# Sums of squared activations stored by the first MLP product, and the last of seven products moved two products on

## The chip, the cores and the metric

The kernel runs on one core of a Trainium2 chip as one program. The metric is the device time of one execution in microseconds. The core's engines work at the same time, each through its own instructions in a fixed order: TensorE (PE in the profile) multiplies into eight PSUM banks, VectorE (DVE), ScalarE (ACT) and GpSimd (POOL) do elementwise work, and SyncE (SP) issues nearly all of the DMAs. An instruction starts when everything ahead of it on its engine has been started and its semaphores are reached, so an instruction that waits holds up all that stand behind it on its engine.

## What is computed

Two layers of a trunk on 1024 tokens of width 1024. Each ends in the same squared-ReLU MLP with 4096 hidden features, which is all that the change touches:

```python
def sqrelu_mlp(hn, w1, w2):
    return jnp.square(jax.nn.relu(hn @ w1)) @ w2
...
        hn = modulate(rms_norm(h, norm2_g[layer]), sh2, sc2)
        h = h + g2[:, None, :] * sqrelu_mlp(hn, mlp_w1[layer], mlp_w2[layer])
```

The first layer mixes tokens with a recurrent block, the second with chunked attention. All is float32; the result must be close to that of float32 arithmetic.

## The kernel before

**Precision.** Each float32 operand is split into a high part (rounded by ScalarE to the type that PE multiplies) and a low part (the difference, made by DVE or POOL). A product of two operands is then three matmuls, high by high, high by low and low by high (lines 241 to 243). Each takes a 128 x 128 block of weights and 512 columns.

**Seven products for eight.** Both matrix products of an MLP are cut into 2 x 2 blocks and multiplied with seven block products in place of eight. This takes sums: of the weight blocks (four instructions on POOL for each group of four loaded blocks, line 111), of the activations of the first product (made once), and of the hidden activations, the squared ReLUs, for the second product. The hidden sums are called T1 to T4, the blocks used as they are B11, B22, B21 and B12. The list `PROD` gives the order of the seven products: which of the four weight units, which half of it, which moving operand, which of three PSUM banks, and whether the bank starts anew. A bank isn't finished with its first product: each further product adds to what lies in it, after the sum so far has been read out. So product after product in a bank has to wait for the read of the one before.

**First product.** Features come in 16 pairs of 128-feature blocks. Pairs 0 and 1 are multiplied plainly, pairs 2 to 15 by the function `quad`, with 4 blocks to a product, 84 matmuls to a pair. ScalarE copies the first three reads of a bank out, DVE adds and squares the rest (lines 998 to 1004). The four finished half tiles of a pair (B11 and B12 side by side in one tile, `ca`, and B21 and B22 in the other, `cb_`) go to DRAM, to the array `hid`, in two DMAs of 512 KB (line 944), issued while the next pair is worked on.

**Second product.** 16 steps, listed in `STEPS`: three short ones of one, two and three pairs, then 13 of four pairs each, every time `quad` with the hidden activations as moving operand. Each step needs a new group of weights, and each full step one new pair of `hid`. The stream of loads fetches that pair in two DMAs of 512 KB, lets ACT and DVE split B11 and B22, lets POOL make T3, T1 and T2 in place (line 359), splits those and B21, and then has POOL make T4. After every product DVE adds the bank, scaled, to the residual `h` (line 1027). A tail of plain products closes what the steps leave.

**What sets the order.** `Stream` holds all weight and `hid` loads in one list. It loads as far as seven raw tiles of 512 KB (`ws`) allow, and splits as far as eight tiles of split weights (`wh`) and a number of operand tiles (`cap["a"]`, up to 30) are free; `pump` is called when a unit is done. All operands, the tiles `ca` and `cb_` and the residual share 38 tiles (`s`). The residual is out of these tiles during the first product and comes back with `reload`, 512 KB each (line 987): blocks 2 to 5 while pairs 8 to 11 are worked on, 6, 7, 0 and 1 at its end. The function `some` puts loads for the modulation vectors of later stages (512 KB each, `in_ada` and `in_kvada`, with one long DVE instruction, line 274) among the units, in the first layer only. A scheduler places the instructions of each engine when the kernel is built, so the fixed order of an engine is seen in the built program and not in the source.

## Time and profile before

| | us |
|---|---|
| runs: median (lowest to highest) of three | 2520.14 (2513.54 to 2522.19) |
| the profiled execution, its own time | 2512.75 |
| its span, first to last instruction | 2511.0 |
| first product of layer 0, the seven-product part | about 640 to 855 |
| second product of layer 0 | about 855 to 1180 |
| first product of layer 1 | about 1950 to 2155 |
| second product of layer 1 | about 2155 to 2500 |

Engines over the span: PE 2323.5 us busy (93%), DVE 1821.6 (73%), ACT 1114.5 (44%), POOL 1112.0 (44%). A busy PE is not PE at its full pace, since matmuls overlap and their ends are modelled; the number of matmuls in a stretch says more. Where nothing holds PE, a matmul of 512 columns starts every 0.226 us.

### The profile page before, as it was taken

The numbers are of one execution on the slowest core, as the hardware profiler recorded it, in microseconds if no ns is written. First come the engines' busy times: TensorE is split into PE (matmuls) and PEld (weight loads), VectorE is DVE, ScalarE is ACT, GpSimd is POOL, SyncE is SP. The second block draws the span as 40 slices with busy tenths as digits, with TensorE's granted clock in tenths as the row PEclk, the third lists the DMA queues.
The fourth block names the chain that finished last, engine by engine and source line by source line (L and its number), as shares of the span: only waits on it lengthen the run. The fifth ranks groups of instructions, "written<-read, shape, count | busy, mean of one in ns | idle before, by whom it ended". The sixth has DMA issues, their size and how long they took to land.

```text
span 2511.0 us, 31516 instructions
## 1 busy us (share of the span) xinstructions
PE 2323.5 (93%) x11764; PEld 1941.9 (77%) x11764; DVE 1821.6 (73%) x2328; ACT 1114.5 (44%) x1808; POOL 1112.0 (44%) x767
## 2 busy tenths in 40 slices
PE   4989888989999989899999999999999999999998
PEld 3767666867888767667799998998887888677777
DVE  8879888678766798776765557997386655887674
ACT  5567665244333333333444218997153333443331
POOL 3535335346343366553211027875046332566550
PEclk9989987999999999999999999999999999999999
DMA  7323344223554543334333300013213342533332
GB/s 292 115 81 83 103 138 151 75 72 118 178 191 167 172 152 121 114 122 139 126 118 126 102 5 12 12 35 112 99 34 125 116 141 101 172 101 102 100 105 93
DMA packets 103402, 283.74 MB, mean 113 GB/s; under 512 B 12016, under 2 KB 17264, under 8 KB 103248
## 3 DMA queue, kind: packets, MB, share of 16 engines
q1 hardware_dynamic: 101952, 277.40, 33.6%
q10 hardware_dynamic: 1296, 4.33, 0.5%
q8 instruction: 92, 1.51, 0.3%
q14 instruction: 62, 0.51, 0.1%
HBM read 219.82 MB, written 50.33 MB: 108 GB/s over the span
## 4 chain that ended last, share of the span: by engine, by line
PE 48%; DVE 22%; DMA 9%; ACT 8%; POOL 7%; issue 6%; SPq 0%; POOLq 0%; DVEq 0%; ACTq 0%
PE b L242 15%; PE b L243 14%; PE b L241 14%; DMA ws<-hid 5%; POOL ws L359 5%; DVE s L175 4%; DMA ws<-in_ada_dram 2%; DVE wl L175 2%; DVE s L1027 2%; POOL ws L111 2%; DVE ws L274 2%; ACT s L174 1%; PE b L1334 1%; ACT s L1304 1%; DVE s L274 1%
## 5 line engine op out<-in xcount | busy, mean ns | idle before, releaser
L242 PE MATMUL b<-s,wh 128*128 128x512 f32 x2540 | 1008.6, 398 | 62.8 <-DVE s L247 35.1
L241 PE MATMUL b<-s,wh 128*128 128x512 f32 x2540 | 995.8, 399 | 65.6 <-DVE s L1027 39.2
L243 PE MATMUL b<-s,wl 128*128 128x512 f32 (+1 forms) x2312 | 911.5, 397 | 12.4 <-DVE wl L175 12.3
L241 PEld LDWEIGHTS b<-s,wh 128*128 128x128 f32 x2540 | 481.6, 190 | 202.1 <-DVE s L1027 56.2
L242 PEld LDWEIGHTS b<-s,wh 128*128 128x128 f32 x2540 | 484.0, 191 | 180.4 <-DVE s L247 38.3
L243 PEld LDWEIGHTS b<-s,wl 128*128 128x128 f32 (+1 forms) x2312 | 440.3, 190 | 113.8 <-DVE wl L175 17.4
L111 POOL TENSOR_TENSOR ws<-ws,ws 128x512 f32<-128x512 f32 (+3 forms) x180 | 283.1, 1573 | 489.0 <-DMA ws<-in_w_dram 277.9
L174 ACT ACTIVATE wh<-ws 128x1024 fp32r<-128x1024 f32 (+4 forms) x324 | 303.5, 941 | 356.8 <-PE b L243 165.4
L175 DVE TENSOR_TENSOR wl<-ws,wh 128x1024 fp32r<-128x1024 f32 (+3 forms) x224 | 301.4, 1348 | 110.5 <-PE b L242 54.9
L174 ACT ACTIVATE s<-ws 128x512 fp32r<-128x512 f32 x230 | 136.5, 626 | 374.9 <-POOL ws L359 244.2
L175 DVE TENSOR_TENSOR s<-ws,s 128x512 fp32r<-128x512 f32 x230 | 199.2, 885 | 137.8 <-ACT s L174 137.0
L241 PE MATMUL b<-wh,s 128*128 128x256 f32 x768 | 216.7, 284 | 4.3 <-ACT s L473 2.2
L243 PE MATMUL b<-wh,s 128*128 128x256 f32 x768 | 213.2, 284 | 5.3 <-DVE s L474 5.1
L242 PE MATMUL b<-wl,s 128*128 128x256 f32 x768 | 216.7, 284 | 0.0
L359 POOL TENSOR_TENSOR ws<-ws,ws 128x512 f32<-128x512 f32 x96 | 153.1, 1595 | 131.0 <-DVE s L175 128.5
L1027 DVE SCALAR_TENSOR_TENSOR s<-b,mod,s 128x512 f32<-128x512 f32 x248 | 181.4, 741 | 37.1 <-PE b L243 37.1
L175 POOL TENSOR_TENSOR wl<-ws,wh 128x1024 fp32r<-128x1024 f32 (+2 forms) x40 | 106.2, 2660 | 218.0 <-ACT wh L174 218.0
L274 DVE CUSTOM_DVE_ANT_0 ws<-ws,cb,vec 128x1024 f32<-128x1024 f32 x68 | 101.8, 1501 | 94.9 <-DMA ws<-in_ada_dram 94.9
L241 PEld LDWEIGHTS b<-wh,s 128*128 128x128 f32 x768 | 147.8, 193 | 5.1 <-ACT s L473 2.9
L243 PEld LDWEIGHTS b<-wh,s 128*128 128x128 f32 x768 | 145.7, 193 | 6.3 <-DVE s L474 5.7
L242 PEld LDWEIGHTS b<-wl,s 128*128 128x128 f32 x768 | 147.8, 193 | 0.2 <-issue 0.2
L274 DVE CUSTOM_DVE_ANT_0 s<-s,cb,vec 128x1024 f32<-128x1024 f32 x44 | 79.2, 1826 | 36.1 <-DMA s<-in_ada_dram 31.0
(173 smaller groups left out, 3246.5 us busy)
## 6 DMA issues: line engine op xcount, KB each, us to landing
ws<-in_w_dram SPq DMA_DIRECT2D x216, 256.0 KB
hid<-s SPq DMA_DIRECT2D x64, 512.0 KB
ws<-hid SPq DMA_DIRECT2D x64, 512.0 KB
ws<-in_ada_dram SPq DMA_DIRECT2D x56, 512.0 KB
s<-in_ada_dram SPq DMA_DIRECT2D x40, 512.0 KB
ws<-in_w_in_dram SPq DMA_DIRECT2D x22, 512.0 KB
hsp<-s SPq DMA_DIRECT2D x32, 256.0 KB
s<-hsp SPq DMA_DIRECT2D x16, 512.0 KB
```

The source lines that it names most:

```text
L111: G.tensor_tensor(out=out, in0=in0, in1=in1, op=op)
L174: nc.scalar.activation(out=hi[:rows, :n], in_=src, func=AF.Copy)
L175: self.lo_engine.tensor_tensor(out=lo[:rows, :n], in0=src, in1=hi[:rows, :n].bitcast(F32), op=ALU.subtract)
L241: PE.matmul(ps, ah, bh, start=start, stop=False, skip_group_check=more)
L242: PE.matmul(ps, ah, bl, start=False, stop=False, skip_group_check=more)
L243: return PE.matmul(ps, al, bh, start=False, stop=stop, skip_group_check=more).ins
L274: V.tensor_tensor_reduce(out=t, in0=t, in1=cb, op0=ALU.mult, op1=ALU.add, scale=1.0, scalar=bias, accum_out=dst)
L359: G.tensor_tensor(out=out, in0=in0, in1=in1, op=ALU.subtract)
L1027: V.scalar_tensor_tensor(out=t, in0=ps, scalar=g2[:, m : m + 1], in1=t, op0=ALU.mult, op1=ALU.add)
L1304: A_.activation(out=p[:, lo:640], in_=p[:, lo:640], func=AF.Exp, scale=-1.0, bias=m, accum_out=s1)
L1334: PE.transpose(ps[:, x, e * 128 : (e + 1) * 128], ptile[e][:, col : col + 128], ident)
```

## The change

It has four parts.

1. **The sums are made where the activations are made.** `hid` has eight blocks for a pair in place of four. When the last product of a pair is read, the two tiles go to DRAM as they are; then POOL makes T3, T1, T2 and T4 in place with the same four subtractions, and both tiles go to DRAM again. So a pair is stored with four DMAs of 512 KB. The second product loads the seven operands of a pair in four DMAs, three of 512 KB with two operands each and one of 256 KB, and splits each as it comes, without a POOL instruction between.
2. **The order of the seven products.** B21 comes ahead of T3, and the last product, T4, is held back: class `Quads` does it after the first two products of the next pair or step.
3. **Engines.** For the pairs 0 to 3 in the second product POOL and not DVE makes the low parts of the loads that end with T3 and T4.
4. **Placement.** Only blocks 2 and 3 of the residual come back during the first product, at pairs 10 and 11; six are fetched at its end. The twelve `some` loads in the second product are in the twelve steps from the second full one on; before, three of them were in the three short steps.

```diff
-        (1, 1, "B22", 1, False), (2, 0, "T3", 0, False), (2, 1, "B21", 2, True),
+        (1, 1, "B22", 1, False), (2, 1, "B21", 2, True), (2, 0, "T3", 0, False),
         (3, 0, "T4", 0, False)]
+
+HID = ["B11", "T2", "T1", "B22", "B21", "T3", "T4", "B12"]
+HLOADS = [("B11", "T1"), ("T2", "B22"), ("B21", "T3"), ("T4",)]
...
-            self.lo_engine.tensor_tensor(out=lo[:rows, :n], in0=src,
-                                         in1=hi[:rows, :n].bitcast(F32), op=ALU.subtract)
+            (it["eng"] or self.lo_engine).tensor_tensor(
+                out=lo[:rows, :n], in0=src, in1=hi[:rows, :n].bitcast(F32), op=ALU.subtract)
...
-    hid = dp.tile([16, 128, 4, HALF], F32, name="hid")
+    hid = dp.tile([16, 128, 8, HALF], F32, name="hid")
...
     def pair(p):
...
+        its = []
+        for nms in HLOADS:
+            i, n = HID.index(nms[0]), len(nms)
+            d = HID.index(nms[-1]) - i if n > 1 else 1
+            src = hid[p][:, i : i + d * (n - 1) + 1 : d]
+            its.append(ws.item([(0, n * HALF, src)], [(x * HALF, HALF, True) for x in range(n)],
+                               to="a", eng=G if p < 4 and nms[-1] in ("T3", "T4") else None))
+        return its
...
-            if j:
+            if p0 > 0:
                 some(1)
...
+        def end(self):
+            if self.late is not None:
+                late, self.late = self.late, None
+                self.product(6, *late)
+
+        def step(self, *a):
+            a = (a[0], [bank() for _ in range(3)], *a[1:])
+            for x in range(6):
+                self.product(x, *a)
+                if x == 1:
+                    self.end()
+            self.late = a
...
-            for t, x in ((ca, 0), (cb_, 2)):
-                nc.sync.dma_start(hid[p][:, x : x + 2], t.rearrange("p (a b) -> p a b", a=2))
+            f = "p (a b) -> p a b"
+            nc.sync.dma_start(hid[p][:, 0:8:7], ca.rearrange(f, a=2))
+            nc.sync.dma_start(hid[p][:, 3:5], cb_.rearrange(f, a=2))
+            a, b = hs(0), hs(1)
+            for out, in0, in1 in ((cb_[:, a], ca[:, b], cb_[:, a]), (ca[:, b], ca[:, b], ca[:, a]),
+                                  (ca[:, a], ca[:, a], cb_[:, a]), (cb_[:, b], cb_[:, b], ca[:, a])):
+                G.tensor_tensor(out=out, in0=in0, in1=in1, op=ALU.subtract)
+            nc.sync.dma_start(hid[p][:, 1:3], ca.rearrange(f, a=2))
+            nc.sync.dma_start(hid[p][:, 5:7], cb_.rearrange(f, a=2))
...
-            def after(x):
-                if x == 1 and stored is not None:
-                    store(*stored)
+            def after(x, p=p, ca=ca, cb_=cb_):
+                if x == 6:
+                    store(p, ca, cb_)
...
-            if p in (8, 9, 10, 11):
-                reload(p - 6)
-        store(*stored)
+            quads.step([ws.next() for _ in range(4)], 4, nrm.op, read, after)
+            if p in (10, 11):
+                reload(p - 8)
+        quads.end()
         ws.cap["a"] = 30
         ws.pump()
-        for k in (6, 7, 0, 1):
+        for k in (4, 5, 6, 7, 0, 1):
             reload(k)
```

Three places show how the instructions move. In the changed kernel the line numbers differ: 113 is the weight sums (111 before), 142 the loads of the stream (137), 953 the subtractions in `store` (359 in `pair` before), 948 and 949 the stores of a pair's two tiles as they are (944), 954 and 955 their second stores, 998 the reload (987), 177 the low parts (175). A name such as `ws110_4538` is a tile and its number; `ws` are the raw loaded tiles.

**POOL in the first product.** Before, eight instructions in a row that are two groups of weight sums:

```order
L111 TENSOR_TENSOR ws110_4538<-ws111_4540,ws108_4535 128x512
L111 TENSOR_TENSOR ws108_4535<-ws111_4540 128x512
L111 TENSOR_TENSOR ws109_4537<-ws110_4538,ws111_4540 128x512
L111 TENSOR_TENSOR ws109_4537<-ws110_4538,ws109_4537 128x512
L111 TENSOR_TENSOR ws116_4673<-ws117_4675,ws114_4670 128x512
L111 TENSOR_TENSOR ws114_4670<-ws117_4675 128x512
L111 TENSOR_TENSOR ws115_4672<-ws116_4673,ws117_4675 128x512
L111 TENSOR_TENSOR ws115_4672<-ws116_4673,ws115_4672 128x512
```

Now, in the same stage (`s522` and `s523` are `ca` and `cb_` of one pair):

```order
L953 TENSOR_TENSOR s523_4625<-s522_4624,s523_4625 128x512
L953 TENSOR_TENSOR s522_4624<-s522_4624 128x512
L953 TENSOR_TENSOR s522_4624<-s522_4624,s523_4625 128x512
L953 TENSOR_TENSOR s523_4625<-s523_4625,s522_4624 128x512
L113 TENSOR_TENSOR ws128_5004<-ws129_5006,ws126_5001 128x512
L113 TENSOR_TENSOR ws126_5001<-ws129_5006 128x512
L113 TENSOR_TENSOR ws127_5003<-ws128_5004,ws129_5006 128x512
L113 TENSOR_TENSOR ws127_5003<-ws128_5004,ws127_5003 128x512
L953 TENSOR_TENSOR s530_4766<-s529_4765,s530_4766 128x512
```

Between one group of weight sums and the next there stand now the four subtractions of a pair, the first of which waits for that pair's tiles to have landed in DRAM.

**POOL in the full steps of the second product.** Before, the sums of the hidden pair (line 359) and those of the weights are interleaved:

```order
L359 TENSOR_TENSOR ws230_7104<-ws229_7085,ws230_7104 128x512
L111 TENSOR_TENSOR ws226_7058<-ws227_7080,ws226_7058 128x512
L359 TENSOR_TENSOR ws229_7085<-ws229_7085 128x512
L359 TENSOR_TENSOR ws229_7085<-ws229_7085,ws230_7104 128x512
L359 TENSOR_TENSOR ws230_7104<-ws230_7104,ws229_7085 128x512
L111 TENSOR_TENSOR ws233_7210<-ws234_7232,ws231_7109 128x512
L111 TENSOR_TENSOR ws231_7109<-ws234_7232 128x512
```

Now only the weight sums are left, step after step:

```order
L113 TENSOR_TENSOR ws211_6540<-ws212_6559,ws209_6501 128x512
L113 TENSOR_TENSOR ws209_6501<-ws212_6559 128x512
L113 TENSOR_TENSOR ws210_6536<-ws211_6540,ws212_6559 128x512
L113 TENSOR_TENSOR ws210_6536<-ws211_6540,ws210_6536 128x512
L113 TENSOR_TENSOR ws220_6693<-ws221_6713,ws218_6654 128x512
```

**SP and POOL where the first product gives way to the second.** Before, on SP (`s575` and `s576` are the last pair's tiles, `hsp` is the residual in DRAM):

```order
L944 DMA hid_86<-s575_5556 128x1024
L137 DMA ws164_5731<-in_w2_dram 128x384
L137 DMA ws166_5734<-in_w2_dram 128x384
L137 DMA ws167_5775<-in_w2_dram 128x384 x2
L944 DMA hid_86<-s576_5557 128x1024
L137 DMA ws168_5790<-hid_86 128x1024
L137 DMA ws169_5804<-hid_86 128x1024
L137 DMA ws170_5812<-in_kvada_dram 128x1024
L987 DMA s594_5752<-hsp324_2446 128x1024
```

Now, on SP (`s573` and `s574` are the last pair's tiles, `s567` the second tile of the pair before it):

```order
L955 DMA hid_86<-s567_5476 128x1024
L998 DMA s592_5838<-hsp324_2446 128x1024
L998 DMA s593_5840<-hsp324_2446 128x1024
L142 DMA ws168_5810<-in_w2_dram 128x384
L998 DMA s594_5842<-hsp324_2446 128x1024
L998 DMA s595_5844<-hsp324_2446 128x1024
L998 DMA s596_5846<-hsp324_2446 128x1024
L998 DMA s597_5848<-hsp324_2446 128x1024
L142 DMA ws169_5865<-in_w2_dram 128x384 x2
L142 DMA ws170_5880<-hid_86 128x2x512
L949 DMA hid_86<-s574_5623 128x1024
L142 DMA ws171_5888<-hid_86 128x2x512
```

And on POOL at the same place (`ws166` to `ws169` are the weights of the step with three pairs, `s605` to `s607` low parts of pair 2's B21, T3 and T4):

```order
L113 TENSOR_TENSOR ws168_5810<-ws169_5865,ws166_5772 128x384
L113 TENSOR_TENSOR ws166_5772<-ws169_5865 128x384
L953 TENSOR_TENSOR s574_5623<-s573_5622,s574_5623 128x512
L953 TENSOR_TENSOR s573_5622<-s573_5622 128x512
L953 TENSOR_TENSOR s573_5622<-s573_5622,s574_5623 128x512
L113 TENSOR_TENSOR ws167_5806<-ws168_5810,ws169_5865 128x384
L177 TENSOR_TENSOR s605_5898<-ws172_5896,s605_5898 128x512
L953 TENSOR_TENSOR s574_5623<-s574_5623,s573_5622 128x512
L177 TENSOR_TENSOR s606_5901<-ws172_5896,s606_5901 128x512
L177 TENSOR_TENSOR s607_5906<-ws173_5904,s607_5906 128x512
L113 TENSOR_TENSOR ws167_5806<-ws168_5810,ws167_5806 128x384
```

The store of the last pair's second tile now stands on SP behind six reloads, and the last two weight sums of the three-pair step stand on POOL behind the last pair's subtractions, which wait for that store to have landed.

More of the change, by code (lines that the diff above doesn't have):

```diff
@@ L1044, in after @@
                     ws.free("a", n)
-            quad([ws.next() for _ in range(4)], p1 - p0, mov, lambda x, ps: add(*spots[x], ps),
-                 after)
+            quads.step([ws.next() for _ in range(4)], p1 - p0, mov,
+                       lambda x, ps, spots=spots: add(*spots[x], ps), after)
+        quads.end()
         its = [ws.next() for _ in range(3)]
```

77 lines of the change are left out of this document (28 added, 49 removed).

## The prediction

> **What bounds the kernel now.** I read the busy time of PE by stretches first, then the waits, then the groups of one stretch. The stretches (us, PE busy and matmuls, granted clock, DMA share, GB/s) of the two MLPs:
>
> ```profile
> 640.00:840.00 200.00, 200.00 (x884) 1.00 0.51 177
> 840.00:930.00 90.00, 78.60 (x309) 0.95 0.49 161
> 930.00:1180.00 250.00, 225.18 (x955) 1.00 0.38 122
> 1950.00:2140.00 190.00, 190.00 (x840) 1.00 0.35 121
> 2140.00:2230.00 90.00, 80.00 (x333) 1.00 0.47 151
> 2230.00:2470.00 240.00, 222.40 (x946) 0.99 0.31 98
> ```
>
> The first product (rows 1 and 4) is dense: 200/884 = 0.2262 us for a matmul. At that pace the matmuls of the other rows would need 69.9, 216.0, 75.3 and 214.0 us; what is over is 20.1 and 34.0 us in layer 0 and 14.7 and 26.0 in layer 1, together 94.8 us. The first of each pair is the boundary of the two products, the second the full steps. So nothing can be won in the first product, and at most 95 us (3.8%) in the second. The waits from 860 to 1170 (total, times, longest) say why:
>
> ```profile
> ACT s L174 <- POOL ws L359: 123.6, 39, 7.3
> POOL ws L359 <- DVE s L175: 60.7, 24, 4.9
> DVE s L175 <- ACT s L174: 56.9, 38, 4.5
> ACT s L174 <- DMA ws<-hid: 55.5, 18, 6.3
> PE b L241 <- DVE s L1027: 24.8, 23, 2.3
> ```
>
> PE waits for DVE's additions (last row), and these are late because they stand on DVE behind splits (line 175) that wait for ACT, which waits for POOL's hidden sums (line 359), which wait for DVE again. The groups from 930 to 1180 (count, busy, mean ns, idle before) show that no engine is full:
>
> ```profile
> L175 DVE TENSOR_TENSOR s<-ws,s 128x512 fp32r<-128x512 f32 x81 | 67.4, 848 | 58.1 <-ACT s L174 58.1
> L1027 DVE SCALAR_TENSOR_TENSOR s<-b,mod,s 128x512 f32<-128x512 f32 x81 | 59.4, 741 | 0.0
> L175 DVE TENSOR_TENSOR wl<-ws,wh 128x1024 fp32r<-128x1024 f32 x34 | 49.5, 1457 | 0.6 <-ACT wh L174 0.6
> L274 DVE CUSTOM_DVE_ANT_0 ws<-ws,cb,vec 128x1024 f32<-128x1024 f32 x8 | 14.2, 1775 | 0.0
> L175 DVE TENSOR_TENSOR wh<-ws,wh 128x512 fp32r<-128x512 f32 x12 | 12.2, 1016 | 0.0
> L359 POOL TENSOR_TENSOR ws<-ws,ws 128x512 f32<-128x512 f32 x34 | 56.1, 1650 | 45.0 <-DVE s L175 44.1
> L359 POOL TENSOR_TENSOR ws<-ws 128x512 f32<-128x512 f32 x11 | 17.6, 1603 | 0.3
> ```
>
> **Full steps of the second product.** The four hidden sums, (56.1 + 17.6)/11.25 = 6.6 us of POOL for a step, leave, and with them the ring DVE - ACT - POOL. What stays on DVE in a step: seven splits 5.9, seven additions 5.2, three long weight splits 4.4, a short one 1.0, in layer 0 one modulation row 1.8: 18.3 us, against 84 x 0.2262 = 19.0 us of PE. It fits, barely in layer 0, well in layer 1 (16.5). A bank's next product now comes two products, 24 matmuls or 5.4 us, after every read, where it was one, 2.7 us; an addition takes 0.74, so it may stand behind three splits and not hold PE. Against it: loads of `hid` grow from 1 to 1.75 MB a step, 0.75/19 us = 39 GB/s on top of 122; row 1 shows 177 carried without harm. I take 4 us left in each layer (nothing is left if DVE never blocks; with 1.5 us of blocking on a late load it passes 19.0 by 0.8, so 10 us over 12 steps), and 60 - 8 = 52 us gained.
>
> **First product.** POOL gets the four subtractions of a pair there, 28 pairs in the steps, and each pair two stores more. Groups from 640 to 840, then the last loads of a group as SP issued them and POOL's first sum after them (start, us):
>
> ```profile
> L111 POOL TENSOR_TENSOR ws<-ws,ws 128x512 f32<-128x512 f32 (+1 forms) x30 | 53.8, 1792 | 118.3 <-DMA ws<-in_w_dram 116.3 <-DVE wl L175 1.2
> ...
> L111 POOL TENSOR_TENSOR ws<-ws 128x512 f32<-128x512 f32 (+1 forms) x10 | 13.5, 1351 | 0.7 <-DMA ws<-in_w_dram 0.7
> ```
>
> ```profile
> 724.13 2.01 SPq L137 DMA_DIRECT2D ws<-in_w_dram  x3
> ```
>
> ```profile
> 728.88 1.76 POOL L111 TENSOR_TENSOR ws<-ws,ws 128x512 f32<-128x512 f32 x1 [11.57 <-DMA ws<-in_w_dram]
> ```
>
> Three instructions of 1.79 and one of 1.35 make 6.7 us for a group of sums, and as much for the subtractions: 13.4 of 19.0 us, so POOL isn't full. But a ring appears: subtractions, second store on SP, the weight loads behind it, the weight sums, and only then the next pair's subtractions. Its length: 6.7 + 6.7, from issue to sums 728.88 - 724.13 = 4.75 (3.7 if issued without gaps, 0.33 each), and the two stores of 512 KB ahead of the loads, 1.3 to 3.1 us at 338 GB/s (row below). That is 18.4 to 21.3 us against 19.0. I take 19.6, near the middle: 0.6 late a step, 8 us after 13 steps. About 7 of them are hidden: T4 ends three products (8.2 us) into a step, its read, the first stores and the subtractions take 2 + 4 + 6.7, the loads behind them 6, which is 8 us into the next step; two sums and the split (3.1 + 2.2) end at 13, and PE needs them at 19. I count 5 us lost over both layers, bounds 0 and 45 (2.3 us late a step in both). Apart from this, T4 at the side of the next pair costs nothing: the matmuls are the same, and its weights are the one `wh` tile of eight that seven others leave free.
>
> **The boundary.** Here three modulation loads leave (1.5 MB), and the hidden sums of the first pairs. What comes is the queue shown ahead: SP issues six reloads (3.1 MB, before 2.1) and only then the last pair's second tile. The drain rate of a full queue, and what a wait does to the clock:
>
> ```profile
> 870.00:880.00 10.00, 9.94 (x37) 7.65 (x36) 10.00 (x14) 4.69 (x9) 5.00 (x5) 0.84 0.71 232
> 880.00:890.00 10.00, 7.90 (x25) 5.30 (x24) 10.00 (x12) 2.83 (x5) 7.94 (x5) 0.83 0.92 338
> ```
>
> ```profile
> 867.86 1.04 PE L241 MATMUL b<-s,wh 128*128 128x512 f32 x2 [1.99 <-ACT s L174]
> ...
> 869.92 0.63 PE L243 MATMUL b<-s,wl 128*128 128x512 f32 x1
> ...
> 872.91 0.55 PE L242 MATMUL b<-s,wh 128*128 128x512 f32 x1
> ```
>
> Let zero be where PE would end the last T4 undelayed. From the previous pair's second stores, issued about 2 us ahead of zero, to the last tile there are 6.4 MB in SP's order (2 x 0.5 of stores, the ready tile 0.5, reloads 3.1, weights 0.6, `hid` 0.5, the tile 0.5): 19 us at 338 GB/s, so with some 2 us of start and finish it lands at about 19. POOL then makes three subtractions (4.9), the third weight sum (1.5), three low parts and the fourth subtraction (6), the fourth sum (1.3): 33. ACT (0.9) and DVE (1.2) split it: 35. PE needs that weight 68 matmuls after zero, at 15.4. So the boundary costs 20 us in a layer; the half speed after the last wait (seven starts 0.43 apart between the two last rows above, in place of 0.23) would add 1.4, which is within the rounding of this chain. Bounds: 9 if the reloads were drained ahead, 40 if the queue drains at 232 GB/s as from 870 to 880, in 28 us, and nine POOL instructions take 2.3 us as below. I take 20: the rate is from the nearest full queue. Now it costs 20.1 and 14.7, so the boundary gives nothing in layer 0 and takes 5 in layer 1.
>
> A page bears on this. The Trainium skill, "TensorE: Matmul & The Clock Gate", Part 1, says that the clock falls to half after an idle window of about 3.4 us. The trace shows half speed after a wait of 1.99 us already, so here short waits cost too; by the page only the two long ones would, about 1 us less in a layer.
>
> **Sum.** 94.8 - 2 x 20 - 8 - 5 = 42 us. The profiled execution took 2512.75 (span 2511.0), the runs 2513.54 to 2522.19, median 2520.14; the same 42 us off the median give **2478**.
>
> **Rivals.**
>
> A, *slower: the POOL ring sets the step of the first product.* Place: the subtractions between the weight sums. It decides from 21.4 us on: 2.4 x 13 - 7 = 24 us in each layer, the gain of the rest. For it: POOL and DVE seem to slow each other. The longest weight sum, and one DVE instruction in the dense stretches of layer 0 and of layer 1, twice as long in the second, where by my reading it falls together with POOL's sums:
>
> ```profile
> 709.22 2.37 POOL L111 TENSOR_TENSOR ws<-ws,ws 128x512 f32<-128x512 f32 x1 [10.94 <-DMA ws<-in_w_dram]
> ```
>
> ```profile
> L175 DVE TENSOR_TENSOR wh<-ws,wh 128x512 fp32r<-128x512 f32 x11 | 7.5, 684 | 0.0
> ```
>
> ```profile
> L175 DVE TENSOR_TENSOR wh<-ws,wh 128x512 fp32r<-128x512 f32 x10 | 13.9, 1391 | 0.0
> ```
>
> With subtractions of 2.3 us the ring is 9.2 + 6.7 + 4.5 + 2.2 = 22.6: 3.6 x 13 - 7 = 40 us a layer, 80 - 47 = 33 slower, **2553**. Against it: layer 1 has no modulation loads there, and 1.79 is a mean over such meetings already. Chance 0.08. The Trainium skill, "GPSIMD Engine Reference", Specifications, has POOL share SBUF interfaces with VectorE, in contention with DVE instructions that have two SBUF inputs. The rows agree (both are such instructions); by that rule the work moved is work moved beside DVE's squares and splits, and this rival is what it would come to.
>
> B, *the boundary takes the gain:* 40 us each: 95 - 80 - 8 = 7, **2513**, no change that can be told. For it: the upper bound's two conditions both occur in the trace; against: they would have to meet twice. 0.07.
>
> C, *DVE becomes the bound of the full steps.* Only 0.7 us are left to it in layer 0; with 2 us of blocked time a step in layer 0 and 1 in layer 1 beyond that, 22 us go: about 20 gained, **2500**. Against: the 58 us for which it waits for ACT hung on POOL. 0.13.
>
> D, *the boundary is cheap,* if six reloads drain early: 9 a layer, 95 - 18 - 8 = 69, **2451**. For it: the loads that went with `some`; against: SP's order, which can't let a reload pass. 0.15.
>
> **How the numbers follow.** My forecast has 0.57. 0.3%, or 7.6 us, is about what can be told from no change. Faster are mine, C and D: 0.85; B is the same: 0.07; A is slower: 0.08. The range 2446 to 2508 holds D to C with a few us of either side, leaving out A, B and tails.
>
> **What would show it.** Right: in the full steps over 218 matmuls in 50 us (now 955/250 x 50 = 191), no ACT wait for POOL at hidden operands, POOL about 13 us busy in 19 in the first product and PE still dense there. At the boundary two PE waits of 5 us or more, on weights whose sums stand behind the last pair's subtractions. Wrong: gaps of PE in the first product that recur with the pairs (A); full steps below 210 with DVE over 95% busy (C); a boundary of over 30 us (B) or under 12 (D).

## The result: 1.6% slower, and the profile after

The changed kernel took 2561.34 us (median of four runs, 2556.97 to 2564.88), the kernel before 2521.16 (2513.54 to 2522.98) beside it: a ratio of 1.0164 with a 95% interval of 1.0138 to 1.0191. The prediction said 2478. The two profiled executions have spans of 2511.0 and 2558.3 us, 47.3 apart. The medians are only 40.2 apart: the profiled execution of the kernel before (2512.75 us) is 8 us under the median of its runs, and no stretch below can be named for that part.

Where the 47.3 us lie is read from instructions that both programs have. The rows below are from the timelines of ACT and DVE of the kernel before: pair 14's first copy in layer 0, the first addition of the second full step, the last additions of the layer, and the same three in layer 1 (start, length in us).

```profile
819.83 0.60 ACT L998 ACTIVATE s<-b 128x512 f32<-128x512 f32 x1 [0.27 <-PE b L243]
931.25 0.74 DVE L1027 SCALAR_TENSOR_TENSOR s<-b,mod,s 128x512 f32<-128x512 f32 x1
1222.94 1.40 DVE L1027 SCALAR_TENSOR_TENSOR s<-b,mod,s 128x512 f32<-128x512 f32 x2
2119.66 0.60 ACT L998 ACTIVATE s<-b 128x512 f32<-128x512 f32 x1 [0.27 <-PE b L243]
2226.36 0.74 DVE L1027 SCALAR_TENSOR_TENSOR s<-b,mod,s 128x512 f32<-128x512 f32 x1
2507.18 0.75 DVE L1027 SCALAR_TENSOR_TENSOR s<-b,mod,s 128x512 f32<-128x512 f32 x1 [0.61 <-PE b L243]
```

And the same instructions of the changed kernel:

```profile
868.35 0.60 ACT L1009 ACTIVATE s<-b 128x512 f32<-128x512 f32 x1 [0.32 <-PE b L245]
993.96 0.74 DVE L1037 SCALAR_TENSOR_TENSOR s<-b,mod,s 128x512 f32<-128x512 f32 x1
1278.93 1.40 DVE L1037 SCALAR_TENSOR_TENSOR s<-b,mod,s 128x512 f32<-128x512 f32 x2
2180.58 0.60 ACT L1009 ACTIVATE s<-b 128x512 f32<-128x512 f32 x1 [0.27 <-PE b L245]
2296.51 0.74 DVE L1037 SCALAR_TENSOR_TENSOR s<-b,mod,s 128x512 f32<-128x512 f32 x1
2554.52 0.75 DVE L1037 SCALAR_TENSOR_TENSOR s<-b,mod,s 128x512 f32<-128x512 f32 x1 [0.61 <-PE b L245]
```

The stretches between these rows, and what the change added to each (the last two pairs of a first product, 14 and 15, are counted with the boundary):

| stretch | before, us | changed, us | added, us |
|---|---|---|---|
| up to pair 14 of layer 0 (its first product) | 819.8 | 868.4 | +48.5 |
| boundary of layer 0, with the first full step | 111.4 | 125.6 | +14.2 |
| the other full steps and the tail, layer 0 | 291.7 | 285.0 | -6.7 |
| from there to pair 14 of layer 1 | 896.7 | 901.7 | +4.9 |
| boundary of layer 1 | 106.7 | 115.9 | +9.2 |
| the other full steps and the tail, layer 1 | 280.8 | 258.0 | -22.8 |

So the gain is there, most of it in layer 1, and the loss has one large place, which layer 1 does not share: the first product of layer 0. In layer 1 that product loses 4.6 of the 4.9 us, all of it between the first copies of pairs 2 and 5 (54.9 us against 50.3 before); from there on its pairs are 19.0 us apart, as before. The windows of the changed kernel show the same (us; then busy time and count of PE, PEld, DVE, ACT, POOL; granted clock, DMA share, GB/s):

```profile
640.00:890.00 250.00, 221.88 (x919) 179.78 (x920) 178.46 (x168) 66.12 (x91) 145.15 (x88) 0.94 0.55 189
890.00:994.00 104.00, 83.34 (x305) 63.40 (x304) 72.57 (x87) 37.03 (x62) 57.26 (x44) 0.86 0.66 219
994.00:1246.00 252.00, 235.80 (x1000) 191.48 (x1000) 178.74 (x234) 88.85 (x125) 57.40 (x42) 0.97 0.52 164
1996.00:2200.00 204.00, 204.00 (x902) 168.92 (x901) 136.58 (x118) 64.10 (x86) 139.22 (x89) 1.00 0.49 174
2200.00:2297.00 97.00, 80.81 (x313) 62.30 (x312) 69.78 (x85) 38.30 (x65) 55.53 (x42) 0.90 0.69 228
2297.00:2523.00 226.00, 226.00 (x995) 187.09 (x994) 168.43 (x209) 88.60 (x122) 62.20 (x41) 1.00 0.47 142
```

Rows 4 and 6 are dense, 902/204 = 4.42 and 995/226 = 4.40 matmuls a us, as the dense rows of before (884/200 = 4.42); layer 1's full steps had 946 in 240 us. Row 1 has 919 in 250 us, a sixth less. POOL has 145 of 250 us of work there and 139 of 204 in row 4: it has more to do in the stretch that is dense. The waits from 590 to 885 (total, times, longest):

```profile
DVE s L276 <- DMA s<-in_ada_dram: 73.1, 12, 10.1
PE b L245 <- DVE wl L177: 35.9, 10, 7.2
POOL ws L113 <- DMA ws<-in_w_dram: 32.9, 8, 8.6
POOL s L953 <- DMA hid<-s: 26.3, 9, 3.4
```

PE waits for the low parts of weights from DVE (line 177), and DVE waits for modulation rows: 84.1 us in 14 waits from 590 to 885, the 10.9 us for rows of `in_kvada` included that the list leaves out. In the kernel before DVE had waited for the same rows too, 36.1 us from 590 to 835, with PE's pairs 19.0 us apart from pair 5 on all the same; the larger part of it:

```profile
DVE s L274 <- DMA s<-in_ada_dram: 31.0, 11, 6.3
```

One turn of it in the changed kernel, first SP's queue (the second store of one pair, three weight loads, two rows, the next pair's store, its second store):

```profile
735.45 0.32 SPq L955 DMA_DIRECT2D hid<-s  x1
735.86 1.72 SPq L142 DMA_DIRECT2D ws<-in_w_dram  x3
737.63 0.90 SPq L142 DMA_DIRECT2D s<-in_ada_dram  x2
748.50 0.33 SPq L949 DMA_DIRECT2D hid<-s  x1
...
758.01 0.32 SPq L955 DMA_DIRECT2D hid<-s  x1
```

then DVE and POOL between (start, length, in brackets the idle time ahead and what ended it):

```profile
744.39 2.38 DVE L276 CUSTOM_DVE_ANT_0 s<-s,cb,vec 128x1024 f32<-128x1024 f32 x1 [10.12 <-DMA s<-in_ada_dram]
...
746.70 1.77 DVE L1015 TENSOR_TENSOR s<-s 128x512 f32<-128x512 f32 x1
...
754.58 2.28 DVE L177 TENSOR_TENSOR wl<-ws,wh 128x1024 fp32r<-128x1024 f32 x1
```

```profile
751.17 1.27 POOL L953 TENSOR_TENSOR s<-s,s 128x512 f32<-128x512 f32 x1 [3.25 <-DMA hid<-s]
752.52 1.59 POOL L953 TENSOR_TENSOR s<-s 128x512 f32<-128x512 f32 x1
754.18 3.80 POOL L953 TENSOR_TENSOR s<-s,s 128x512 f32<-128x512 f32 x2
```

The two rows can't be issued before SP has passed the second store, which waits for POOL's last subtraction. DVE starts on the first 6.8 us after their issue, and has stood still for 10.1 us by then, because the row is next in its order. Behind it stand the square that finishes the pair (746.70), the store of that pair (748.50), its landing, for which POOL waits (3.25), and the four subtractions, which release the next second store at 758.01. The ring is 758.01 - 735.45 = 22.6 us long; the turn before, from the second store at 709.86 on, took 25.6. A pair has 84 x 0.2267 = 19.0 us of matmuls. The weight split behind the rows comes at 754.58, and PE stands for 7.0 us at that place, and then runs at half pace (the granted clock is 0.50 from 756 to 762):

```profile
756.91 0.80 PE L245 MATMUL b<-s,wl 128*128 128x512 f32 x1 [7.00 <-DVE wl L177]
...
762.20 0.54 PE L243 MATMUL b<-s,wh 128*128 128x512 f32 x1
762.57 0.39 PE L244 MATMUL b<-s,wh 128*128 128x512 f32 x1
```

### The profile page after: what moved, and what is told of

Its sections match the earlier page's. It is cut to its first block, busy times and chain, and to the rows that moved or that the text cites. A ratio compares the mean times of both kernels' runs of the same rounds, so it can differ in the third digit from the quotient of the medians.

```text
span 2558.3 us, 32000 instructions
## 1 busy us (share of the span) xinstructions
PE 2345.9 (92%) x11764; PEld 1969.8 (77%) x11764; DVE 1839.1 (72%) x2304; ACT 1117.8 (44%) x1808; POOL 1137.7 (44%) x791
## 4 chain that ended last, share of the span: by engine, by line
PE 55%; DVE 18%; DMA 10%; ACT 6%; issue 6%; POOL 4%; SPq 1%; DVEq 0%; POOLq 0%; ACTq 0%
PE b L245 17%; PE b L244 17%; PE b L243 17%; DMA ws<-hid 3%; DMA ws<-in_ada_dram 3%; DVE wl L177 3%; POOL s L953 2%; DVE s L276 1%; ACT s L1314 1%; PE b L1344 1%; DVE ws L276 1%; DVE s L656 1%; DMA s<-in_ada_dram 1%; DVE s L177 1%; ACT s L248 1%
## 5 line engine op out<-in xcount | busy, mean ns | idle before, releaser
L244 PE MATMUL b<-s,wh 128*128 128x512 f32 x2540 | 1020.7, 402 | 58.2 <-DVE s L249 34.8
L243 PE MATMUL b<-s,wh 128*128 128x512 f32 x2540 | 1005.3, 403 | 44.7 <-ACT wh L176 18.9
L244 PEld LDWEIGHTS b<-s,wh 128*128 128x128 f32 x2540 | 491.9, 194 | 174.5 <-DVE s L249 37.7
L243 PEld LDWEIGHTS b<-s,wh 128*128 128x128 f32 x2540 | 490.7, 193 | 167.4 <-ACT wh L176 22.3
L245 PEld LDWEIGHTS b<-s,wl 128*128 128x128 f32 (+1 forms) x2312 | 446.1, 193 | 172.7 <-DVE wl L177 74.7
L113 POOL TENSOR_TENSOR ws<-ws,ws 128x512 f32<-128x512 f32 (+3 forms) x180 | 265.7, 1476 | 506.4 <-DMA ws<-in_w_dram 328.0
L177 DVE TENSOR_TENSOR wl<-ws,wh 128x1024 fp32r<-128x1024 f32 (+3 forms) x224 | 321.0, 1435 | 91.2 <-PE b L244 47.0
L177 DVE TENSOR_TENSOR s<-ws,s 128x512 fp32r<-128x512 f32 x206 | 169.6, 840 | 103.0 <-ACT s L176 102.8
L953 POOL TENSOR_TENSOR s<-s,s 128x512 f32<-128x512 f32 x96 | 161.7, 1685 | 86.2 <-DMA hid<-s 71.5
```

The source lines that it names most:

```text
L113: G.tensor_tensor(out=out, in0=in0, in1=in1, op=op)
L177: (it["eng"] or self.lo_engine).tensor_tensor(out=lo[:rows, :n], in0=src, in1=hi[:rows, :n].bitcast(F32), op=ALU.subtract)
L243: PE.matmul(ps, ah, bh, start=start, stop=False, skip_group_check=more)
L244: PE.matmul(ps, ah, bl, start=False, stop=False, skip_group_check=more)
L245: return PE.matmul(ps, al, bh, start=False, stop=stop, skip_group_check=more).ins
L953: G.tensor_tensor(out=out, in0=in0, in1=in1, op=ALU.subtract)
```

## The experiments

Theory R, formed from the trace above: the ring passes SP, the rows, DVE, the store and POOL. Its rivals: A, the ring of the prediction (subtractions, second stores, weight loads, weight sums), which needs no rows; S, POOL and DVE slow each other, since both have more work; Q, the transfers have become too many. The time before was 2516 to 2518 us beside these runs, and 2521 beside the change. What each kernel adds to the kernel before in the six stretches of the table above, read from its own trace at the same instructions (us), with the median and the ratio to before. A trace is one execution: that of e3 is 9 us under the median of its runs, the others are within 5 of it.

| kernel | product 0 | boundary 0 | steps 0 | to pair 14 of 1 | boundary 1 | steps 1 | median | ratio, interval |
|---|---|---|---|---|---|---|---|---|
| the change | +48.5 | +14.2 | -6.7 | +4.9 | +9.2 | -22.8 | 2561.3 | 1.0164 [1.0138, 1.0191] |
| e1_rows_other | +36.8 | +19.5 | -24.4 | +9.1 | +9.6 | -22.8 | 2536.4 | 1.0073 [1.0056, 1.0090] |
| e2_stores_first | +7.6 | +7.9 | -10.2 | +6.5 | +12.4 | -24.4 | 2514.1 | 0.9989 [0.9975, 1.0002] |
| e3_pool_queue | +28.3 | +14.1 | -11.9 | +7.8 | +12.5 | -21.7 | 2551.1 | 1.0127 [1.0106, 1.0148] |
| e4_old_order | +44.5 | +20.5 | -10.9 | +9.1 | +11.6 | -24.5 | 2558.4 | 1.0167 [1.0149, 1.0185] |
| e5_rows_act | +8.8 | +21.9 | -13.4 | +4.4 | +10.6 | -23.1 | 2524.2 | 1.0031 [1.0020, 1.0042] |
| e6_rows_out | -5.9 | +6.4 | -31.7 | +7.6 | +10.2 | -21.6 | 2476.6 | 0.9835 [0.9817, 0.9853] |
| e7_reload_act | +17.1 | +23.7 | -14.5 | +8.5 | +14.2 | -22.9 | 2539.9 | 1.0096 [1.0079, 1.0113] |
| e8_lows_dve | +9.8 | +12.2 | -12.0 | +5.2 | +6.7 | -22.3 | 2517.6 | 0.9996 [0.9986, 1.0005] |
| e9_pool_stores | +9.9 | -5.2 | -10.2 | +9.3 | +3.4 | -23.6 | 2495.8 | 0.9917 [0.9904, 0.9930] |
| e10_last_dve | +10.8 | -5.0 | -10.1 | +10.6 | +4.2 | -23.5 | 2498.3 | 0.9922 [0.9907, 0.9937] |
| e11_rows_late | +5.7 | -2.4 | -15.1 | +10.5 | +3.3 | -23.6 | 2491.4 | 0.9895 [0.9881, 0.9910] |
| e12_order_alone | -2.0 | +0.9 | +4.0 | +1.6 | +2.7 | +4.3 | 2527.4 | 1.0039 [1.0025, 1.0052] |

### Is the ring closed by SP's wait for POOL?

**e2_stores_first** issues all four stores of a pair ahead of the subtractions, so that the sums are left out of what is stored.

```diff
             nc.sync.dma_start(hid[p][:, 3:5], cb_.rearrange(f, a=2))
+            nc.sync.dma_start(hid[p][:, 1:3], ca.rearrange(f, a=2))
+            nc.sync.dma_start(hid[p][:, 5:7], cb_.rearrange(f, a=2))
...
-            nc.sync.dma_start(hid[p][:, 1:3], ca.rearrange(f, a=2))
-            nc.sync.dma_start(hid[p][:, 5:7], cb_.rearrange(f, a=2))
```

> Left out here: the second stores carry what the first ones carry, since all four stores of a pair are issued ahead of the subtractions; bytes, stores and POOL work stay, but SP no longer waits for POOL. Theory R and rival A: the ring is open, layer 0's first product becomes at most 10 us longer than before the change, about 50 us less, and the full steps of layer 0 still wait for rows: about 2508 (2495 to 2520). Rival S (POOL and DVE slow each other) and rival Q (too many transfers): nothing that sets the time has gone, 2548 to 2568.

2514.1 us. The window of the first product in layer 0 is dense (its columns as above):

```profile
640.00:840.00 200.00, 200.00 (x877) 165.43 (x877) 165.56 (x158) 62.03 (x83) 139.59 (x84) 0.99 0.65 224
```

Every byte and every subtraction is still there, at 224 GB/s in place of 189, with POOL busy 140 of 200 us beside a DVE that is busy 166. So neither the bytes (Q) nor the two engines slowing each other (S) sets the step; in this kernel SP's wait for POOL was what did, as both R and A have it. (e3 below takes the same wait away in another way, and there something else holds most of the time.)

### Do the rows belong to the ring?

**e1_rows_other** was to keep the rows' loads and DVE's work and to take only the wait away.

```diff
+            if t is cb:
+                V.tensor_tensor(out=cb, in0=cb, in1=cb, op=ALU.max)
...
-                    use(its[at]["st"])
+                    use(cb)
```

> Left out here: the 41 modulation rows that belong to layer 0's MLP are still loaded, in the same places of SP's queue, but DVE does not read them; in their place it takes the maximum of a tile that it has long had with itself (128x1024, two inputs), so DVE keeps about the same work and loses only the wait for the load. Theory R (a row's load stands on SP behind the second stores, DVE stands in order behind the row, the last square and the raw store behind DVE, the subtractions behind that store: a ring of 22.6 to 25.6 us a pair against 19.0): layer 0's first product, now 61 us longer than before the change, becomes at most 10 us longer, as layer 1's is, and layer 0's full steps, in which DVE now waits 20.0 us for rows, gain about 20 us: 2558 - 51 - 20 = about 2487 (2470 to 2505). Rival A (subtractions, second store, weight loads, weight sums: a ring without the rows) and rival S (POOL and DVE slow each other) and rival Q (the transfers take too long because there are more of them): within 10 us of the changed kernel, 2548 to 2568.

It measured 2536.4, between the two answers, and is not clean: with nothing to wait for, the scheduler started all 40 of the maxima between 393 and 516 us, ahead of the MLP, so that pair 2's first copy comes at 625.5 us in place of 594.7, 31 us later. Only what follows can be read: from pair 3 to pair 14 the product is dense, and the full steps of layer 0 gain 24.4. That speaks for R; the total decides nothing.

**e5_rows_act** leaves everything as it is and issues the rows from ACT.

```diff
-                self.nc.sync.dma_start(dst, src)
+                (self.nc.scalar if it.get("mlp") else self.nc.sync).dma_start(dst, src)
```

> The changed kernel with one edit: the loads of the 41 modulation rows of layer 0's MLP are issued by ACT's queue in place of SP's. Bytes, DVE work, stores, subtractions and SP's wait for POOL all stay. Theory R (the ring is closed by the rows, which stand on SP behind the second stores): layer 0's first product, now 48.6 us longer than before from pair 3's first copy to pair 14's, becomes at most 10 us longer, and layer 0's full steps gain 24 us on before, as layer 1's do, in place of 8: 2558 - 40 - 15 = about 2503 (2493 to 2515). Rival A (subtractions, second stores, weight loads, weight sums): the ring has no row in it, so 2548 to 2566. Rival T (ACT is held by its issues, because a tile is not free yet): PE waits for ACT's copies and splits, over 2566.

2524.2: 37 us less than the change (33 by the two ratios). Up to pair 14 layer 0 now adds 8.8 us in place of 48.5, which A alone could not give. But it is 20 us more than R expected, in the boundary (+21.9) and the full steps, and the trace shows why for the first of them. The first subtraction of five pairs in a row on POOL:

```profile
758.66 1.30 POOL L954 TENSOR_TENSOR s<-s,s 128x512 f32<-128x512 f32 x1
...
779.05 1.29 POOL L954 TENSOR_TENSOR s<-s,s 128x512 f32<-128x512 f32 x1
...
799.05 1.29 POOL L954 TENSOR_TENSOR s<-s,s 128x512 f32<-128x512 f32 x1
...
820.26 1.29 POOL L954 TENSOR_TENSOR s<-s,s 128x512 f32<-128x512 f32 x1
...
840.62 1.28 POOL L954 TENSOR_TENSOR s<-s,s 128x512 f32<-128x512 f32 x1
```

and what stands between the first two, on SP (second store, three weight loads) and on POOL (weight sums):

```profile
766.15 0.32 SPq L956 DMA_DIRECT2D hid<-s  x1
766.56 3.02 SPq L142 DMA_DIRECT2D ws<-in_w_dram  x3
```

```profile
773.05 1.29 POOL L113 TENSOR_TENSOR ws<-ws,ws 128x512 f32<-128x512 f32 x1 [6.92 <-DVE s L959]
774.29 1.29 POOL L113 TENSOR_TENSOR ws<-ws 128x512 f32<-128x512 f32 x1
775.54 3.55 POOL L113 TENSOR_TENSOR ws<-ws,ws 128x512 f32<-128x512 f32 x2
```

With the rows out of SP's queue the ring of the prediction comes to light, and no row's load stands in it: subtractions end at 766.13, second store at 766.15, weight loads, sums from 773.05 to 779.09, subtractions at once. (The first of these lines names DVE for the wait of 6.92, but that instruction had ended at 772.55; the weight load issued at 768.73 landed at 772.93.) (840.62 - 758.66)/4 = 20.5 us a pair, 1.5 more than PE needs. PE's pairs stay 19.0 us apart up to pair 10 and are 19.4 to 21.6 apart from there to pair 15, as POOL's lag reaches it. So there are two rings on the same wait of SP, R the longer one. DVE isn't out of the second one: from 600 to 860 SP's weight loads wait 25.9 us for DVE, in 28 waits, most of that time for splits, which free the raw tiles, and the rows' work stands on DVE between those splits.

```profile
SPq L142 <- DVE wl L177: 14.6, 13, 4.7
```

**e6_rows_out** leaves the rows out.

```diff
                 src, _n, use = rest.pop(0)
+                continue
...
-                some(1)
+                rest.pop(0)
```

> Left out here: the 41 modulation rows of layer 0's MLP, their loads and their DVE instructions; the vectors that they make are constants. SP still waits for POOL ahead of every second store. Theory R: layer 0's MLP behaves as layer 1's, its first product 2 to 5 us longer than before and its full steps 24 us shorter: 2558 - 45 - 16 = about 2497 (2485 to 2507). Rival A: 2545 to 2566, since subtractions, stores and weight loads stand as they did.

2476.6, 20 us less than expected. Layer 0 is now as layer 1: its pairs are 19.0 us apart from pair 5 on, and its full steps are 31.7 us shorter than before. The -5.9 is no gain of the product itself: pair 2's first copy comes 6.8 us earlier, and from there to pair 14 it takes 0.8 longer than before. A falls as the explanation of the 48.5 us, since SP still waits for POOL ahead of every second store. But POOL's built order is another one here, the same as in layer 1 of the change: two of a group's four weight sums stand ahead of a pair's subtractions and two behind them, and POOL waits 3.3 to 3.8 us for the store's landing at each pair from 5 to 12. So the 20.5 us ring is that of e5's order, with rows on DVE, and not of the stored sums as such. The number is no measure of a better kernel, since before still makes the rows; 31.7 also holds their DVE work in the steps.

**e3_pool_queue** lets POOL issue the second stores, the rows staying on SP.

```diff
-            nc.sync.dma_start(hid[p][:, 1:3], ca.rearrange(f, a=2))
-            nc.sync.dma_start(hid[p][:, 5:7], cb_.rearrange(f, a=2))
+            G.dma_start(hid[p][:, 1:3], ca.rearrange(f, a=2))
+            G.dma_start(hid[p][:, 5:7], cb_.rearrange(f, a=2))
```

> The second stores of a pair are issued by POOL behind its subtractions in place of SP. Theory R and rival A: SP's loads pass them, layer 0's first product becomes dense but for some 10 us, so about 2508 (2490 to 2525), if an issue costs POOL under 2 us; the boundary may gain some us, since the reloads no longer stand behind the last second stores. Rivals S and Q: 2548 to 2568. If an issue holds POOL for 4 us or more, POOL has 13.4 + 8 us and more a step and the first products of both layers lose 20 us each or more: over 2580.

2551.1: a miss for R and A as they were stated. Only 20 of the 48.5 us go. An issue costs POOL 0.54 to 0.59 us, so that isn't it. DVE still stands for rows; on SP these are behind the three weight loads, which wait for raw tiles that DVE frees with its splits (54.0 us in 24 waits from 600 to 860, where the change has 23.6 in 12). So a ring of SP and DVE without POOL is left, by the trace; that reading was not tested by itself.

### The two halves of the change

**e4_old_order** keeps the stored sums and has the products in their old order; **e12_order_alone** has the kernel of before with the new order, T4's place, the store after T4 and the six reloads.

```diff
-            for x in range(6):
-                self.product(x, *a)
-                if x == 1:
-                    self.end()
-            self.late = a
+            for x in range(7):
+                self.product(x, *a)
```

> The sums stay stored as in the change, but the seven products run in the order of before, T3 ahead of B21 and T4 last in its own step. If the order is what made layer 1's full steps dense (28 us gained there), most of that returns as waits of PE for DVE's additions: 2558 + 15 to 30 = 2573 to 2588. If the stored sums alone did it: 2558 within 6, with layer 1's full steps still at 222 matmuls in 50 us. Layer 0's first product keeps its 61 us in either case, since the ring does not hang on the order.

> The other half of the change alone: the kernel of before, its sums made in the second product as there, with the new order of the seven products, T4 held back by two products, a pair stored when T4 has been read, and six reloads at the end of the first product in place of four. If the order hides DVE's late additions by itself (22.0 us of PE's waits in layer 0's full steps of before were on additions): full steps 10 to 20 us shorter in each layer, boundary up to 8 us longer in each: 2517 - 30 + 10 = about 2495 (2485 to 2510). If the ring of hidden sums, ACT and DVE paces the steps whatever the order: full steps within 4 us, 2514 to 2532 with the boundary.

Stored sums in the old order: 2558.4, as the change, with layer 1's full steps 24.5 shorter than before. New order without them: 2527.4, slower than before, its full steps 4 us longer in each layer. So the whole gain of the full steps is that of the stored sums, and the order gives them nothing.

### The boundary, and a version that beats both

The kernels e7 and e8 start from e5, each of e9, e10 and e11 from the one ahead of it.

**e7_reload_act** issues the residual's reloads from ACT too.

```diff
-            nc.sync.dma_start(h[k], nrm.dram[k])
+            nc.scalar.dma_start(h[k], nrm.dram[k])
```

> The kernel with the rows on ACT's queue, and the reloads of the residual on ACT's queue as well. If the boundary's long wait (7.0 us in layer 1, on a weight whose loads SP issued behind the six reloads) is a matter of SP's order: the boundary, now 14.2 and 9.2 us longer than before, gets 5 to 10 us shorter in each layer, 10 to 20 us less than the kernel with the rows alone moved. If the bytes set it (the reloads share the same bandwidth): within 4 us of that kernel. If ACT is held by issues that wait for a free tile: 5 to 20 us more than that kernel.

2539.9, 16 us more than e5, and neither boundary is shorter. ACT's queue is a worse place for the reloads: ACT stands 10.75 us at the one issued at 770.75 and 6.11 at the last ones, and behind that PE waits 6.8 us for a copy and 4.5 for a split. So e7 puts a new wait where it takes one away; it gives SP's order no support and doesn't rule it out.

**e8_lows_dve** gives the low parts of the pairs 0 to 3 back to DVE.

```diff
-                               to="a", eng=G if p < 4 and nms[-1] in ("T3", "T4") else None))
+                               to="a", eng=None))
```

> The kernel with the rows on ACT's queue, and the low parts that the change gave to POOL for pairs 0 to 3 back on DVE. If POOL's queue sets the boundary (subtractions, low parts and weight sums in one row): each of two waits in a layer gets up to 4 us shorter, 6 to 14 us less than the kernel with the rows alone moved. If DVE is as tight there: within 4 us, or up to 8 us more, with additions later.

2517.6, 6.6 less than e5; the two boundaries are 9.7 and 3.9 us shorter and the other stretches a little longer: POOL's list of work counts there. What is left, PE's longest wait from 860 to 960:

```profile
PE b L243 <- ACT s L1010: 14.1, 1, 14.1
```

The copy that ends it is the last of these three of ACT:

```profile
871.13 1.67 ACT L176 ACTIVATE s<-ws 128x512 fp32r<-128x512 f32 x3 [10.17 <-DMA ws<-hid]
...
878.87 0.63 ACT L176 ACTIVATE s<-ws 128x512 fp32r<-128x512 f32 x1 [5.29 <-DMA ws<-hid]
879.41 0.58 ACT L1010 ACTIVATE s<-b 128x512 f32<-128x512 f32 x1
```

It stands in ACT's order behind splits of `hid` loads, and the loads of the first were issued from 864.87 on, right behind two second stores that had waited for POOL (862.76 and 864.45): once more a load behind such a store, an engine that takes it in order, and PE's work behind that.

**e9_pool_stores** adds e3's edit, the second stores on POOL's queue.

> Rows on ACT's queue, the low parts of pairs 0 to 3 on DVE, and now the second stores on POOL's queue. With the rows alone moved, a ring of subtractions, second stores, weight loads and weight sums was left, 20.5 us a pair (POOL's first subtractions at 758.66, 779.05, 799.05, 820.26, 840.62), against 19.2 of PE. If that ring is closed by SP's wait for POOL, it opens here: the start of layer 0's first product (11.0 us longer than before) and its end (boundary 12.2 longer) lose 10 to 16 us together, so 2517 - 13 = about 2504 (2498 to 2510). If it is POOL's own time (subtractions, sums and 1.1 us for two issues), nothing is gained, 2515 to 2522, since POOL has more to do.

2495.8, 22 us less than e8 and more than expected, though POOL has more to do; 17.4 of it is in layer 0's boundary, where the 14.1 us wait is gone (PE's only wait for a copy there is 1.8 us). That the lag which the 20.5 us ring builds up over eleven pairs had come out there is a reading. With the ring open POOL's first subtractions are (865.24 - 651.74)/11 = 19.4 us apart, as far as PE's pairs 3 to 14 in this kernel:

```profile
651.74 1.75 POOL L954 TENSOR_TENSOR s<-s,s 128x512 f32<-128x512 f32 x1
...
865.24 1.70 POOL L954 TENSOR_TENSOR s<-s,s 128x512 f32<-128x512 f32 x1 [2.45 <-DMA hid<-s]
```

**e10_last_dve** makes the last pair's sums on DVE.

```diff
-                G.tensor_tensor(out=out, in0=in0, in1=in1, op=ALU.subtract)
+                (V if p == 15 else G).tensor_tensor(out=out, in0=in0, in1=in1, op=ALU.subtract)
```

> The same, and the four subtractions of the last pair, 15, on DVE in place of POOL (0.7 to 1.2 us each there, 1.7 on POOL). If the boundary's long wait is the weight sums behind the last pair's subtractions and low parts on POOL, each boundary gets 4 to 7 us shorter: 8 to 14 us under the kernel without this edit. If the wait is set by the loads behind the reloads on SP: within 3 us of it.

2498.3, the same as e9 within their runs: the last pair's subtractions on POOL don't set the boundary any more.

**e11_rows_late** lets DVE take a row of the full steps no earlier than a step after its load.

```diff
-                ws.add(*rest.pop(0))["mlp"] = True
+                late = [ws.add(*rest.pop(0))]
+                late[0]["mlp"] = True
```

> The same as the kernel with the last pair on DVE, and each row of layer 0's full steps may be read only after the next step's second weight unit has been split, a step later than its load. If DVE's wait for rows is what is left of layer 0's full steps (13.7 us gained there on before, 24 in layer 1): 6 to 10 us under that kernel, all of it there. If the scheduler puts the reads where they were, or the raw tile held longer stops the weight loads: within 3 us, or over it.

2491.4 (2488.1 to 2492.9), 7 us under e10 as expected (4 under e9), though only 5.0 of them in layer 0's full steps. This is the fastest kernel with the whole computation: 1.0% under the kernel before.

## Why the prediction was wrong

**The full steps** were sized at 30 and 22 us of gain. In layer 1 it is 22.8, with PE dense and POOL's ring gone: right, as is POOL's 13 us of work in a pair's 19 beside a dense PE in layer 1's first product (139 of 204). The second reason given, that reads two products away let DVE be late, isn't borne out: e4 gains as much without it. In layer 0 it is 6.7. The step that failed is "4 us left in each layer", with DVE blocking at most 1.5 us a step on late loads. DVE does block, 1.8 us for each row, and PE stands behind it; from 994 to 1246:

```profile
DVE ws L276 <- DMA ws<-in_kvada_dram: 20.0, 11, 2.2
PE b L245 <- DVE wl L177: 16.2, 9, 2.7
```

That wait, and some 7 us of half pace after some of its turns, are most of the 252 - 1000 x 0.2262 = 26 us by which this window is longer than a dense one.

Before, the rows of the full steps had 0.0 us of idle time ahead of them, and the prediction took that over. This is the condition of rival C (2 us of blocked time a step) in one layer; its sign, DVE over 95% busy, did not come (178.74 of 252 us). e5, e11 and e6 (13.4, 15.1 and 31.7 in place of 6.7) show that the rows are the cause; how much is their wait and how much their work in steps that the stored sums have made dense is open.

**The first product** was sized at 5 us over both layers and cost 48.5 in layer 0 alone. The step that failed is the list of the ring: "subtractions, second store on SP, the weight loads behind it, the weight sums". That ring shows in e5, 20.5 us long, within the 18.4 to 21.3 predicted. That is in part luck: subtractions 7.5 and sums 6.0 (6.7 each in the sum), and 6.9 between, about 2 of them SP's wait for DVE, where the sum had the transfer of two stores (1.3 to 3.1; no row gives the 1.3). In layer 1, with POOL's other order, there is no such ring. And two more loads stand behind the same stores, the rows; DVE takes them in order, ahead of the square that finishes the next pair. Prediction and rival A both followed POOL's queue and not DVE's, though the trace of before had DVE standing for these rows, 36.1 us in all. In the ring with the rows the landing of the first store, 3.25 us for which POOL waits, is a link too.

**Rival A** gave 2553, near the truth, for another reason: it had 40 us in each layer from subtractions of 2.3 us. They took 1.69 on average (1.26 to 2.36):

```profile
L953 POOL TENSOR_TENSOR s<-s,s 128x512 f32<-128x512 f32 x96 | 161.7, 1685 | 86.2 <-DMA hid<-s 71.5
```

The Trainium skill, "GPSIMD Engine Reference", Specifications, by which POOL and VectorE contend for SBUF, was named for this rival. e2, with both engines' work in place and PE dense, shows that no such contention sets the time here.

**The boundary** was to cost nothing more in layer 0 and 5 us in layer 1; it cost 14.2 and 9.2. By the windows, 104 - 305 x 0.2262 = 35 and 97 - 313 x 0.2262 = 26 us of PE are over, where 20 were forecast; the first is past the sign of rival B. Two waits of 5 us or more were forecast in each; there is one in layer 0 (5.1) and one in layer 1 (7.0), and several of 2 to 4.5. The chain given for it, reloads ahead of the last tile and then POOL, has no support: e7 moves the reloads and loses (to a new wait of ACT), and on top of e9, where the boundary is cheap already, moving the last subtractions (e10) changes nothing. What moved it, on top of e5, is POOL's low parts (e8) and SP's wait for POOL (e9).

**The sum.** -42 was forecast and +47 came between the two profiled executions (+40 between the medians), 89 us off: 43 in layer 0's first product (48.5 against 5), 23 in its full steps (6.7 against 30), 18 at the boundaries (23.4 against 5), and 5 from layer 0's last addition to pair 14 of layer 1, which is layer 1's first product. The reason is one for the first two: all of it is in the layer that has rows. Rivals B and D leave out the 5 us of the first product that the forecast counts; with it they are 2 and 64 us of gain in place of 7 and 69.

The Trainium skill, "DMA: Bandwidth & Descriptors", Issuing engines are not separate DMA queues, says that issuing from several engines only saves the sequencer's issue time, usually small. Here two rows take 0.9 us to issue, and moving the 40 from SP to ACT saved 37 us of the kernel: what is saved is the wait behind the store ahead of them in SP's order.

What is left open: some 6 to 10 us that layer 0 still loses up to pair 14 in e5 and e8 to e11 but not in e6 (about 6.4 of them lie between the first copies of pairs 2 and 5, 60.2 to 60.4 us against 53.8 before and 54.7 in e6), and what holds e3.

## What to carry to other kernels

When a DMA that waits for an engine is put into a shared queue, list everything behind it in that queue and follow each load to the engine that takes it in order, until the chain comes back; the longest of these rings sets the step, and an engine with two fifths of its time free (POOL here) can be a link of it. Put such a store on the queue of the engine that it waits for, and the loads on another: here the stores alone gave 10 us of the median (e3), the loads alone 37 (e5), and the stores on top of e8 22 more (e9). A second copy of the stage without some of the loads, as layer 1 here, is the first place to compare, and a wait that costs nothing before, as DVE's for the rows, is the first to put into the sum.

## What was not expected of the hardware

A wait of PE costs more than its length. Up to pair 14 of layer 0 PE stood for 36.3 us, 3.9 before. After each of its six waits of 2.5 us or more matmuls came 0.43 us apart in place of 0.23, 59 in all, another 12 us; the first matmuls after a wait, up to 0.60 apart, make up most of the rest of the 48.5. The prediction had 1.4 us for it. After the wait of 7.0 us shown above the slow stretch lasted 5.7 us, to 762.57. The Trainium skill, "TensorE: Matmul & The Clock Gate", Part 1, has the clock fall after an idle window of about 3.4 us that runs freely; in layer 0's full steps 7 matmuls came 0.43 us apart after a wait of 2.06 us (at 1120.50), and none after one of 2.49 (at 1056.69), so the length of the wait alone does not decide, and shorter ones than a window count.
